# V of the first 256 tokens in float32 from unnormalised tokens, and dt beside V in one product

## The chip, the cores and the metric

The kernel runs on one core of a Trainium2 chip. The metric is the device time of one execution in microseconds: before the change 1092.85 us, the median of three runs (1092.71 to 1092.87).

## What is computed

The reference is one layer of an encoder trunk with 512 tokens of width 1024, in float32: a mixing sub-layer and an MLP, each between RMSNorms. The change touches only the beginning of the first sub-layer:

```python
h = rmsnorm(x, pre_mix_norm[l])          # x * rsqrt(mean(x*x) + EPS) * gain, per token
proj = h @ w_in[l]                       # 1024 x 9792
z, xbc, dt_raw, q, k, v, gates = split_cols(proj, IN_SPLITS)
...
dt = jax.nn.softplus(dt_raw.astype(jnp.float32).reshape(Bsz, S, 2, G, R)
                     + dt_bias.astype(jnp.float32).reshape(2, G, R))
...
out = jnp.einsum('bngrqk,bnkgd->bnqgrd', p.astype(v.dtype), vb)
```

v has 256 columns, dt 64 (32 heads in each of two directions). A token's norm is one number per token, and the gain one per input channel.

## The kernel before, in words

**Splitting.** Most products run on TensorE in float32r, a faster form with fewer bits. To keep float32's accuracy each operand is split into a high part (a cast, ACT, L495) and a low part (the rest, POOL or DVE, L499), and `mm3` (L426) adds three products: high with high, high with low, low with high. A plain float32 product (`mm` with float32 operands) is recorded as two weight loads and two MATMUL records. h, the normalised tokens transposed to channels x tokens, is kept split, as eight pairs of tiles of 128 channels x 512 tokens.

**Quanta.** `build` (L1596) lists the work of TensorE as quanta, each with its chunks of weights. `prefetch` (L503) issues a chunk's load from SP (L475) and its split (L495, L499) some chunks ahead: raw weights (`wr`) have 3 buffers, split ones (`wh`, `wl`) have 3. Functions set at a quantum's index (`at`, `later`) are emitted between quanta. At the end `chain` (L519) hands all instructions to a planner, which goes through them with estimated costs and due times and fixes the order on each engine; within an engine, the order of the built program is kept by the hardware. Loads issued from SP go through eight completion semaphores (shared with ACT's two at the start), so the ninth waits until the first has landed.

**The start** (`start`, L591). ACT issues the loads of the identity (`ident`) and the gain (`g`). TensorE does 18 products of a zero tile (`WARM`) that nothing reads, then turns the gain into a column `gT`. `start_tokens` (L620) loads a group of tokens, sums their squares (ACT L635 and DVE L636, half each), takes the inverse root on POOL (L638, L639), scales them (ACT L640, DVE L641), transposes them on TensorE (L424 through `tr`), and splits them with the gain into h (ACT L445, DVE L446). It is called for token group 0 (a group is 128 tokens) at once, with six more unread products (`DUMMY`, x with itself), for group 1 and for groups 2 and 3 together a little later. Loads on SP stand in this order: group 0, the two chunks of V's weights (512 KB each), groups 1, 2 and 3, dt's weights, `vec`, `hot`, K's first weights, the constants `cst`, and so on.

**V, dt, K.** `tm` (L567) makes four quanta for V, one per token group, each 24 split products 256 wide, with tokens as the output's rows; `v_done` copies two groups at once into V. Then `dt_quantum` (L722): dt's 64 columns, high and low part side by side as 128 columns, times both parts of h (16 products 512 wide), gives dt as columns x tokens; a quantum later four float32 products with a folding matrix (`cst,dtr`) turn it back and add the parts; `dt_math` (L746) adds the bias and goes on. Then two quanta for K (24 split products 512 wide each, `cm` L548), and Q. `vectors` (L685) and `bias_rows` (L704) put two transposes and one float32 product (`ps<-hot,vec`) between.

Of the kernel before, what the change touches and what calls it, by code (L numbers as in the profile page):

```python
# [10 lines left out]
F32 = mybir.dt.float32  # L11
# [20 lines left out]
FAR, AHEAD = (2,3,5,6,8,9,11,12,), 5  # L32

BACK = 3
WARM = 18
DUMMY = 6
COLD = 7000.0
RATE, LAND = 260, 2500

# [39 lines left out]
class Slots:  # L79
# [13 lines left out]
    def put(self, *tiles):  # L93
        for t in tiles:
            self.free.append(self.slot.pop(id(t))[0])
# [266 lines left out]
class Trunk:  # L362
# [169 lines left out]
    def run_quanta(self):  # L532
        c = released = 0
        for self.now, q in enumerate(self.quanta):
            n = len(q.chunks)
            self.prefetch(released + SPL + RAW - 2, SPL, released)
            self.emit(self.now)
            q.run([self.parts.pop(c + i) for i in range(n)])
            self.emit(self.now + 0.5)
            c += n  # L540
            released += q.release
        self.now += 1
        while self.acts:
            self.now = min(self.acts)
            self.emit(self.now)
        self.chain()
# [17 lines left out]

        return Quantum(chunks, run)

    def tm(self, c, done):  # L567

        src = lambda k0: self.d_w_in[k0 * 128:(k0 + 4) * 128, c:c + 256].rearrange("(k p) n -> p k n", p=128)
        chunks = [(src(k0), 4, 256, "vpvp") for k0 in (0, 4)]  # L570
        held, ps = [], []

        def step(t):
            def run(parts):
                held.extend(parts)
                if t % 2 == 0:
                    ps.append(self.bank("ps"))
                tok = slice(t * 128, (t + 1) * 128)
                for k in range(8):
                    wh, wl = held[k // 4]  # L580
                    h = self.h[k]
                    self.mm3(ps[-1][:, t % 2 * 256:t % 2 * 256 + 256], (h[0][:, tok], h[1][:, tok]),
                             (wh[:, k % 4], wl[:, k % 4]), k == 0, k == 7)
                if t % 2:
                    done(t // 2, ps[-1])
            return run

        return [Quantum([] if t else chunks, step(t), 2 if t == 3 else 0) for t in range(NT)]


    def start(self):  # L591
        nc = self.nc
        get, put = self.slots.get, self.slots.put
        self.ident = self.const("ident", [128, 128])
        nc.scalar.dma_start(self.ident, self.d_cst[:, :128])
        g = get("g", (128, 128))
        nc.scalar.dma_start(g[:8], self.d_pre_mix_norm[0].rearrange("(k p) -> k p", p=128))
        self.mhalf = self.const("mhalf", [128, 1])
        nc.vector.memset(self.mhalf, -0.5)
# [3 lines left out]
        zero = get("zero", (128, 128))  # L603
        nc.vector.memset(zero, 0.0)
        pg = self.bank("ps")
        for _ in range(WARM):
            self.mm(pg[:, 128:256], zero, zero, True, True)
        put(zero)
        self.tr(pg[:, :8], g[:8, :])
        nc.vector.tensor_copy(self.gT, pg[:, :8])  # L610
        put(g)
        self.dummy = self.bank("ps")
        self.h = [(get("h", dtype=F32R), get("h", dtype=F32R)) for _ in range(8)]
        self.start_tokens([0])
        self.prefetch(2, 1)
        self.at(1, lambda: self.start_tokens([1]))
        self.at(2, lambda: self.start_tokens([2, 3]))
        self.at(1, self.later_constants)

    def start_tokens(self, ts):  # L620

        nc = self.nc
        get, put = self.slots.get, self.slots.put
        n = len(ts)
        ps = [self.bank("pp" if 0 in ts else "ps") for _ in range(2 * n)]
        at = lambda k, i=0, j=n: ps[k % (2 * n)][:, (k // (2 * n) * n + i) * 128:(k // (2 * n) * n + j) * 128]
        xs = {t: [get("x") for _ in range(2)] for t in ts}
        for t in ts:
            for j, x in enumerate(xs[t]):
                nc.sync.dma_start(x, self.d_x[0, t * 128:(t + 1) * 128, j * 512:(j + 1) * 512])  # L630
        for i, t in enumerate(ts):
            xt = xs[t]
            junk = [get("junk") for _ in range(2)]
            ssq, r = self.ssq0[:, 2 * t:2 * t + 2], self.rst0[:, t:t + 1]
            nc.scalar.activation(junk[0], xt[0], AF.Square, scale=D ** -0.5, accum_out=ssq[:, 0:1])  # L635
            nc.vector.tensor_tensor_reduce(junk[1], xt[1], xt[1], 1.0 / D, EPS, ALU.mult, ALU.add, ssq[:, 1:2])  # L636
            put(*junk)
            nc.gpsimd.tensor_tensor(r, ssq[:, 0:1], ssq[:, 1:2], op=ALU.add)  # L638
            nc.gpsimd.tensor_tensor(r, r, self.mhalf, op=ALU.pow)  # L639
            nc.scalar.activation(xt[0], xt[0], AF.Copy, scale=r)  # L640
# [3 lines left out]
            if t == 0:  # L644
                for _ in range(DUMMY):
                    self.mm(self.dummy[:, :128], xt[1][:, :128], xt[1][:, :128], True, True)
# [57 lines left out]
    def bias_rows(self):  # L704

        nc = self.nc
        get, put = self.slots.get, self.slots.put
        hot = get("hot")
        nc.sync.dma_start(hot[:33], self.d_hot)
        ps = self.bank("ps")  # L710
        self.mm(ps[:16, :], self.vec[:33, 256:], hot[:33], True, True)
        rows = get("rows")
        nc.vector.tensor_copy(rows[:16], ps[:16, :])
        self.brow = self.dp.tile([16, 512], F32, name="brow")
        nc.sync.dma_start(self.brow, rows[:16])
        put(hot, rows, self.vec)
        self.row = self.const("row", [128, 176])
        self.bcast_row(self.row, self.d_row, 176)
        self.sink = self.row[:, 128:144]


    def dt_quantum(self):  # L722


        w = self.d_w_in

        def run(parts):
            ps = self.bank("pp")
            for k in range(8):
                for i, h in enumerate(self.h[k]):  # L730
                    self.mm(ps, parts[0][:, k], h, k + i == 0, k + i == 8)
            raw = self.slots.get("dtr")
            self.nc.scalar.copy(raw, ps)

            def flip():
                pt = self.bank("ps")
                for t in range(NT):
                    self.mm(pt[:, t * 64:(t + 1) * 64], raw[:, t * 128:(t + 1) * 128], self.fold, True, True)
                self.slots.put(raw)
                self.dt_math(pt)  # L740

            self.later(1, flip)

        return Quantum([(w[:, C_DT:C_DT + 64].rearrange("(k p) n -> p k n", p=128), 8, 64, "both")], run)

    def dt_math(self, ps):  # L746
# [6 lines left out]
        w = [get("dtw", (128, 4, 64)) for _ in range(6)]  # L753
        v, e, r, s2, p, al = w
        nc.vector.tensor_tensor(v, ps[:, :256].rearrange("p (c h) -> p c h", c=4),
                                bias[:, 0].unsqueeze(1).to_broadcast([128, 4, 64]), op=ALU.add)

        nc.scalar.activation(e, v, AF.Abs)
        nc.scalar.activation(e, e, AF.Exp, scale=-1.0)
# [49 lines left out]
    def kv_quanta(self):  # L809
        nc = self.nc  # L810
        get = self.slots.get
        self.KH, self.KL, self.V = [], [], []

        def k_done(ps):
            for j in range(2):
# [7 lines left out]
                self.KH.append(KH)  # L823
                self.KL.append(KL)

        def v_done(t2, ps):
            V = get("V", (128, 2, 256))
            nc.scalar.copy(V, ps.rearrange("p (t c) -> p t c", t=2))
            self.V.append(V)

        hh = lambda: self.h
        return self.tm(C_V, v_done) + [self.cm(self.d_w_in, C_K + 128 * i, hh, k_done) for i in range(2)]

    def backward(self, ap):

# [760 lines left out]
    def build(self):  # L1596
# [5 lines left out]
        self.at(4, self.vectors)  # L1602
        self.at(4, self.bias_rows)
        self.at(8, self.scan_constants)
# [73 lines left out]
```

## Time and profile before

| | |
|---|---|
| median of three runs | 1092.85 us (1092.71 to 1092.87) |
| profiled execution, first to last instruction (span) | 1090.1 us |
| TensorE busy (PE) | 1080.1 us, 99% |
| VectorE, ScalarE, GpSimd busy | 740.1, 642.9, 794.5 us |
| moved by DMA | 132.31 MB, 121 GB/s in the mean |

The profile gives no time of its own for the profiled execution beyond the span; the difference of 2.75 us between span and median lies before the first and after the last instruction. PE is TensorE's products, PEld its weight loads, DVE VectorE, ACT ScalarE, POOL GpSimd, SP the queue that issues nearly all loads. In a timeline row stand start, length, engine, line, operation, output<-inputs, form and count, and in brackets the idle time of the engine before it and what ended it. The length of a matmul record runs from its start to its modelled end, so back-to-back records overlap; the step between starts is what one costs. Tile names carry no buffer numbers: `h<-pp,gT` is the split of h, `wr` raw weights, `wh` and `wl` their parts.

### The profile page before, as it was taken

How to read it: one execution, taken by the hardware profiler on the slowest of the kernel's cores; microseconds unless marked ns; L12 is line 12 of the kernel's file. 1: busy time of each engine (PE TensorE's matmuls, PEld its weight loads, DVE VectorE, ACT ScalarE, POOL GpSimd, SP SyncE). 2: the span in 40 equal slices, each digit the busy share in tenths (PEclk: the TensorE clock that was granted, in tenths of full speed). 3: DMA queues.
4: the chain of work that ended last, by engine and by line, in shares of the span. 5: the costliest groups of instructions: out<-in, count | busy, mean ns of one | idle time of the engine just before them, and what ended most of it. 6: DMA issues, size and time to landing. Idle time of an engine off the chain costs nothing.

```text
span 1090.1 us, 16770 instructions
## 1 busy us (share of the span) xinstructions
PE 1080.1 (99%) x5631; PEld 906.1 (83%) x5631; DVE 740.1 (68%) x1288; ACT 642.9 (59%) x1379; POOL 794.5 (73%) x977
## 2 busy tenths in 40 slices
PE   9999999999999999999999999999999999999997
PEld 8888888888888888888888888889888888888885
DVE  5567788687788687778788753334672583583698
ACT  6566777686776777676769633323554544544552
POOL 3546657557668888988999876521588898898994
PEclk9999999999999999999999999999999999999998
DMA  7434433634354536354655554534322422424222
GB/s 205 127 95 129 117 94 95 157 90 118 100 123 127 145 101 174 97 141 134 162 138 140 145 173 121 165 103 155 92 70 71 153 74 83 154 74 147 90 97 77
DMA packets 209209, 132.31 MB, mean 121 GB/s; under 512 B 10538, under 2 KB 192042, under 8 KB 209123
## 3 DMA queue, kind: packets, MB, share of 16 engines
q1 hardware_dynamic: 208963, 131.18, 42.6%
q8 instruction: 44, 0.72, 0.3%
q14 instruction: 42, 0.34, 0.1%
q10 hardware_dynamic: 160, 0.07, 0.0%
HBM read 126.69 MB, written 4.52 MB: 120 GB/s over the span
## 4 chain that ended last, share of the span: by engine, by line
PE 98%; DVE 0%; DMA 0%; ACT 0%; issue 0%; POOL 0%; DVEq 0%; POOLq 0%; SPq 0%
PE pp L420 69%; PE ps L420 25%; PE ps L424 3%; DMA rb<-csT 0%; DVEq L1674 0%; DVE ag L1586 0%; DVE h L446 0%; POOLq L1674 0%; ACT h L445 0%; ACT wh L495 0%; SPq L1101 0%; PE pp L424 0%; POOL ssq L1164 0%; ACT x L640 0%; DVE acc L1564 0%
## 5 line engine op out<-in xcount | busy, mean ns | idle before, releaser
L499 POOL TENSOR_TENSOR wl<-wr,wh 128x256 fp32r<-128x256 f32 (+1 forms) x504 | 426.0, 873 | 153.5 <-ACT wh L495 141.7
L420 PE MATMUL pp<-h,wh 128*128 128x512 f32 (+1 forms) x1728 | 527.9, 388 | 0.0
L420 PEld LDWEIGHTS pp<-h,wh 128*128 128x128 f32 x1728 | 318.9, 188 | 64.1 <-issue 1.9
L420 PE MATMUL pp<-h,wl 128*128 128x512 f32 (+1 forms) x856 | 332.3, 388 | 0.0
L495 ACT CAST wh<-wr 128x1024 fp32r<-128x1024 f32 (+1 forms) x133 | 138.9, 1044 | 144.6 <-PE pp L420 125.2
L420 PEld LDWEIGHTS pp<-h,wl 128*128 128x128 f32 x856 | 160.9, 188 | 32.5 <-issue 0.5
L1512 POOL TENSOR_TENSOR wl<-wd,wh 128x256 fp32r<-128x256 f32 x158 | 131.1, 865 | 11.7 <-ACT wh L1509 11.6
L1509 ACT CAST wh<-wd 128x512 fp32r<-128x512 f32 x82 | 47.5, 621 | 32.8 <-PE ps L420 15.5
L420 PE MATMUL ps<-wl,fh 128*128 128x512 f32 x164 | 63.9, 390 | 0.0
L420 PE MATMUL ps<-wh,fl 128*128 128x512 f32 x164 | 63.8, 389 | 0.0
L420 PE MATMUL ps<-wh,fh 128*128 128x512 f32 x164 | 63.8, 389 | 0.0
L1379 DVE SCALAR_TENSOR_TENSOR pp<-pp,r 128x512 f32<-128x512 f32 (+1 forms) x31 | 17.6, 567 | 66.3 <-ACT r L1376 66.3
L1120 ACT ACTIVATE n<-cb,tables 128x128 f32<-128x128 f32 x128 | 49.5, 394 | 17.1 <-DVE cb L1111 16.6
L952 DVE SCALAR_TENSOR_TENSOR u<-pp,cv,u 128x510 f32<-128x510 f32 (+1 forms) x64 | 47.7, 745 | 4.5 <-ACT u L948 3.4
L420 PE MATMUL pp<-yh,wl 128*128 128x512 f32 x128 | 49.8, 390 | 0.0
L420 PE MATMUL pp<-yh,wh 128*128 128x512 f32 x128 | 49.7, 389 | 0.0
L420 PE MATMUL pp<-yl,wh 128*128 128x512 f32 x128 | 49.6, 389 | 0.0
L1121 ACT ACTIVATE m<-cb,tables 128x128 f32<-128x128 f32 x128 | 49.3, 393 | 0.3 <-DVE cb L1111 0.2
L1116 ACT ACTIVATE rf<-rf,tables 128x128 f32<-128x128 f32 x128 | 42.7, 396 | 11.2 <-DMA rf<-csT 11.1
L1156 POOL TENSOR_TENSOR w<-w,E 128x256 f32<-128x256 f32 x48 | 37.9, 803 | 13.1 <-DVE w L1152 11.8
L1050 POOL TENSOR_TENSOR xd<-x,tables 128x256 f32<-128x256 f32 x48 | 33.0, 705 | 17.8 <-ACT x L975 12.8
L884 ACT ACTIVATE P<-P,mx 128x384 f32<-128x384 f32 (+1 forms) x64 | 35.3, 554 | 15.6 <-DVE mx L881 15.3
(271 smaller groups left out, 2163.1 us busy)
## 6 DMA issues: line engine op xcount, KB each, us to landing
wr<-in_w_in SPq DMA_DIRECT2D x76, 512.0 KB, 4.0
wr<-in_w_mlp_in SPq DMA_DIRECT2D x32, 512.0 KB, 4.2
wd<-in_w_mlp_out SPq DMA_DIRECT2D x64, 256.0 KB, 6.3
rf<-csT SPq DMA_DIRECT2D x32, 256.0 KB, 4.8
rb<-csT SPq DMA_DIRECT2D x32, 256.0 KB, 3.7
wr<-in_w_ssd_out SPq DMA_DIRECT2D x14, 512.0 KB, 3.9
E<-csE SPq DMA_DIRECT2D x96, 64.0 KB, 4.2
x<-in_x SPq DMA_DIRECT2D x16, 256.0 KB, 4.2
```

The costliest lines, as they stand in the source:

```text
L420: self.nc.tensor.matmul(out, lhsT, rhs, start=start, stop=stop, skip_group_check=more)
L495: self.nc.scalar.copy(hi[:, :m], raw)
L499: engines[e].tensor_tensor(lo[:, c], raw[:, c], hi[:, c].bitcast(F32), op=ALU.subtract)
L884: nc.scalar.activation(p[:, :w], p[:, :w], AF.Exp, bias=mx[:, n:n + 1], accum_out=sm[:, n:n + 1])
L952: nc.vector.scalar_tensor_tensor(u[:, a:e], ps[:, a + d:e + d], self.wtap(t, b), u[:, a:e], op0=ALU.mult, op1=ALU.add)
L1050: nc.gpsimd.tensor_tensor(v4(xd[:, d * 256:(d + 1) * 256]), v4(xs(c)), by_dir(self.coef, c)[:, d].unsqueeze(2).to_broadcast([128, 4, 64]), ...
L1116: nc.scalar.activation(v4(rf)[:, h], v4(rf)[:, h], AF.Identity, bias=ncs[:, 0, h:h + 1])
L1120: nc.scalar.activation(v4(n)[:, h], cb[:, 0], AF.Copy, scale=dt[:, 0, h:h + 1])
L1121: nc.scalar.activation(v4(m)[:, h], cb[:, 1], AF.Copy, scale=dt[:, 1, h:h + 1])
L1156: nc.gpsimd.tensor_tensor(wc, wc, E[:, d], op=ALU.add)
L1509: nc.scalar.copy(hi, src)
L1512: (nc.vector if q == 512 else nc.gpsimd).tensor_tensor(lo[:, c], src[:, c], hi[:, c].bitcast(F32), op=ALU.subtract)
```

## The change

V and dt now share one set of weights: three chunks of 2, 3 and 3 blocks of 128 channels, each with V's 256 and dt's 64 columns side by side (320 wide), loaded by two DMAs.

Token groups 0 and 1 are transposed raw (`raw_tokens`), and their eviction from PSUM multiplies only by the gain, into `xg`. Their V and dt are plain float32 products, `xg` with the unsplit weights, 16 in all, 320 wide; the token's inverse norm is applied when V and dt are evicted (`done`: ACT for V, DVE for dt, with the bias). Group 1's transposes are issued between the first chunk's products for group 0 and those for group 1. The weights are split as well (ACT the high part, DVE and POOL the low part in turns), for groups 2 and 3.

h of groups 0 and 1, which K, Q and all others need, is made later by `scale_tokens`: two products of a matrix of ones with a diagonal of the inverse norms give a tile with the norms along the row; DVE multiplies `xg` by it (eight times, 256 wide), ACT casts the high part, POOL subtracts the low part.

Groups 2 and 3 go through `start_tokens` as before, and their V and dt are 48 split products 320 wide. dt comes out with tokens as rows, so that `dt_quantum`, its flip and its 64 columns times 512 tokens are gone. `WARM` goes from 18 to 6, on a tile of ones, and `DUMMY` away. The load of `row` (dt's bias among others) moves ahead of `vec` and `hot`; the loads of group 1 move ahead of the second and third chunk of weights. The first call of `prefetch` takes one raw chunk fewer.

In the changed program's order on ACT, group 1's V eviction stands ahead of the scaling of group 3, and the eight splits of groups 2 and 3 ahead of the cast of K's first weights; on POOL the eight low parts of groups 0 and 1 stand between the four subtractions of K's first weights.

```diff
-WARM = 18
-DUMMY = 6
+WARM = 6
+V_CHUNKS = ((0, 2), (2, 5), (5, 8))
...
-            self.prefetch(released + SPL + RAW - 2, SPL, released)
+            self.prefetch(released + SPL + RAW - 2 - (self.now == 0), SPL, released)
...
+    def v_quanta(self):
...
+            def loads():
+                r = self.wp.tile([128, 1024], F32, tag="wr", name=self.name("wr"), bufs=RAW)
...
+                for c, n, at in ((C_V, 256, 0), (C_DT, 64, 256)):
+                    nc.sync.dma_start(raw[0][:, :, at:at + n],
+                                      w[k0 * 128:k1 * 128, c:c + n].rearrange("(k p) n -> p k n", p=128))
+
+            def make():
+                hi, lo = (t[:, :kk * 320].rearrange("p (k n) -> p k n", k=kk) for t in self.weight_parts())
+                nc.scalar.copy(hi, raw[0])
+                for k in range(kk):
+                    e = nc.vector if k % 2 == 0 else nc.gpsimd
+                    e.tensor_tensor(lo[:, k], raw[0][:, k], hi[:, k].bitcast(F32), op=ALU.subtract)
+                return raw[0], hi, lo
...
+        def done(t, ps):
+            bias = self.row[:, :64]
+            if t < 2:
+                r = self.rst0[:, t:t + 1]
+                nc.scalar.activation(self.V[0][:, t], ps[:, :256], AF.Copy, scale=r)
+                nc.vector.scalar_tensor_tensor(self.dtv[:, t], ps[:, 256:320], r, bias, op0=ALU.mult, op1=ALU.add)
+            else:
+                nc.scalar.copy(self.V[1][:, t - 2], ps[:, :256])
+                nc.vector.tensor_tensor(self.dtv[:, t], ps[:, 256:320], bias, op=ALU.add)
...
+        def plain(parts):
...
+            for (k0, k1), (raw, _, _) in zip(V_CHUNKS, parts):
+                for t in range(2):
+                    if (k0, t) == (0, 1):
+                        self.raw_tokens(1)
+                    for k in range(k0, k1):
+                        self.mm(ps[t][:, :320], self.xg[k][:, tok(t)], raw[:, k - k0], k == 0, k == 7)
...
+        def rest(c):
+            def run(_):
...
+                for t in (2, 3):
+                    for k in range(k0, k1):
+                        hi, lo = self.h[k]
+                        self.mm3(late[t - 2][:, :320], (hi[:, tok(t)], lo[:, tok(t)]), (wh[:, k - k0], wl[:, k - k0]),
+                                 k == 0, k == 7)
...
+    def raw_tokens(self, t):
...
+        for k in range(8):
+            self.tr(ps[k // 4][:, k % 4 * 128:(k % 4 + 1) * 128], xt[k // 4][:, k % 4 * 128:(k % 4 + 1) * 128])
+        for k in range(8):
+            dst, src = self.xg[k][:, t * 128:(t + 1) * 128], ps[k // 4][:, k % 4 * 128:(k % 4 + 1) * 128]
+            if k < 4:
+                nc.scalar.activation(dst, src, AF.Copy, scale=self.gT[:, k:k + 1])
+            else:
+                nc.vector.tensor_scalar(dst, src, self.gT[:, k:k + 1], None, op0=ALU.mult)
+        self.token_scale(t, xt)
...
+    def scale_tokens(self, ones, xg):
...
+        for t in range(2):
+            dg = get("dg", (128, 128))
+            nc.gpsimd.tensor_scalar(dg, self.ident, self.rst0[:, t:t + 1], None, op0=ALU.mult)
+            self.mm(rb[:, t * 128:(t + 1) * 128], ones, dg, True, True)
...
+        for k in range(8):
+            x = hf[k // 2][:, k % 2 * 256:(k % 2 + 1) * 256]
+            nc.vector.tensor_tensor(x, rb[:, :256], self.xg[k], op=ALU.mult)
+            hi, lo = (a[:, :256] for a in self.h[k])
+            nc.scalar.copy(hi, x)
+            nc.gpsimd.tensor_tensor(lo, x, hi.bitcast(F32), op=ALU.subtract)
...
-        kv = self.kv_quanta()
-        self.add(*kv[:4], self.dt_quantum(), *kv[4:])
+        self.add(*self.v_quanta(), *self.kv_quanta())
```

More of the change, by code (lines that the diff above doesn't have):

```diff
@@ L586, in step @@
             return run
-        return [Quantum([] if t else chunks, step(t), 2 if t == 3 else 0) for t in range(NT)]
+        return [Quantum([chunk(*c) for c in V_CHUNKS], plain, 0)] + [Quantum([], rest(c), 1) for c in range(3)]
     def start(self):
@@ new lines, in token_scale @@
+    def token_scale(self, t, xt):
+        nc = self.nc
+        get, put = self.slots.get, self.slots.put
+        junk = [get("junk") for _ in range(2)]
+        ssq, r = self.ssq0[:, 2 * t:2 * t + 2], self.rst0[:, t:t + 1]
+        nc.scalar.activation(junk[0], xt[0], AF.Square, scale=D ** -0.5, accum_out=ssq[:, 0:1])
+        nc.vector.tensor_tensor_reduce(junk[1], xt[1], xt[1], 1.0 / D, EPS, ALU.mult, ALU.add, ssq[:, 1:2])
+        put(*junk)
+        nc.gpsimd.tensor_tensor(r, ssq[:, 0:1], ssq[:, 1:2], op=ALU.add)
+        nc.gpsimd.tensor_tensor(r, r, self.mhalf, op=ALU.pow)
+        return r
@@ L624, in start_tokens @@
         n = len(ts)
-        ps = [self.bank("pp" if 0 in ts else "ps") for _ in range(2 * n)]
+        ps = [self.bank(tag) for tag in ("pp", "pp", "ps", "ps")]
         at = lambda k, i=0, j=n: ps[k % (2 * n)][:, (k // (2 * n) * n + i) * 128:(k // (2 * n) * n + j) * 128]
[L627 to L630, printed above, removed]
+        xs = [self.load_tokens(t) for t in ts]
         for i, t in enumerate(ts):
[L632 to L639, printed above, removed]
+            xt = xs[i]
+            r = self.token_scale(t, xt)
             nc.scalar.activation(xt[0], xt[0], AF.Copy, scale=r)
@@ L716, in bias_rows, with dt_math @@
         put(hot, rows, self.vec)
[L717 to L746, printed above, removed]
+    def dt_math(self):
         nc = self.nc
@@ L824, in k_done @@
                 self.KL.append(KL)
[L826 to L829, printed above, removed]
         hh = lambda: self.h
[L832 removed]
+        return [self.cm(self.d_w_in, C_K + 128 * i, hh, k_done) for i in range(2)]
     def backward(self, ap):
```

90 lines of the change are left out of this document (54 added, 36 removed).

## The prediction

> **What bounds the kernel now.** I read the page first, then the busy time by stretches, the waits of PE, and the timeline of the first 60 us. From the page: busy time, the clock row, and the chain that ended last.
>
> ```profile
> PE 1080.1 (99%) x5631; PEld 906.1 (83%) x5631; DVE 740.1 (68%) x1288; ACT 642.9 (59%) x1379; POOL 794.5 (73%) x977
> ...
> PEclk9999999999999999999999999999999999999998
> ...
> PE 98%; DVE 0%; DMA 0%; ACT 0%; issue 0%; POOL 0%; DVEq 0%; POOLq 0%; SPq 0%
> ```
>
> TensorE is 99% of the span and 98% of the chain. The stretches show where the last per cent lies (columns: length, then busy time and instructions of PE, PEld, DVE, ACT, POOL; clock; DMA):
>
> ```profile
> 0.00:21.00 21.00, 19.18 (x122) 17.09 (x122) 12.03 (x36) 14.36 (x35) 8.60 (x17) 1.00 0.84 244
> 21.00:70.00 49.00, 49.00 (x256) 41.18 (x256) 29.53 (x63) 28.91 (x56) 23.19 (x32) 1.00 0.39 108
> 70.00:200.00 130.00, 130.00 (x775) 110.82 (x774) 98.97 (x224) 92.30 (x222) 78.89 (x102) 1.00 0.41 111
> 400.00:800.00 400.00, 399.64 (x2024) 334.71 (x2023) 261.44 (x375) 227.40 (x478) 290.49 (x346) 1.00 0.48 135
> ```
>
> From 21 us on PE does not rest. So any PE work taken out, or any earlier start of the useful products, moves the end by as much. Before 21 us much of "busy" is filler:
>
> ```profile
> 1.03 6.64 PE L420 MATMUL ps<-zero 128*128 128x128 f32 x36 [1.03 <-DVE mhalf L599]
> ...
> 8.08 1.04 PE L424 MATMUL pp<-ident,x 128*128 128x128 f32 x8
> 8.95 1.28 PE L420 MATMUL ps<-x 128*128 128x128 f32 x10
> 9.99 0.36 PE L420 MATMUL ps<-wh,h 128*128 128x256 f32 x1
> ```
>
> The first product whose result is used starts at 9.99 us. The start is the whole matter: I compare the time at which the first product of K begins, since nothing but PE work follows it and the two programs have the same products from there.
>
> **That mark in the kernel before.**
>
> ```profile
> 20.75 1.40 PE L420 MATMUL pp<-h,wh 128*128 128x512 f32 x4
> ...
> 23.82 0.40 PE L420 MATMUL pp<-h,wh 128*128 128x512 f32 x1
> ...
> 25.92 0.40 PE L420 MATMUL ps<-wh,h 128*128 128x256 f32 x2
> 26.16 0.28 PE L420 MATMUL ps<-wl,h 128*128 128x256 f32 x1
> 26.28 0.40 PE L420 MATMUL ps<-wh,h 128*128 128x256 f32 x2
> ...
> 29.21 1.03 PE L420 MATMUL ps<-hot,vec 33*16 33x512 f32 x2
> 30.17 3.26 PE L420 MATMUL pp<-h,wh 128*128 128x512 f32 x13
> 33.27 0.39 PE L420 MATMUL pp<-h,wl 128*128 128x512 f32 x1
> ...
> 34.18 0.62 PE L420 MATMUL pp<-h,wh 128*128 128x512 f32 x2
> ...
> 34.86 0.62 PE L420 MATMUL pp<-h,wh 128*128 128x512 f32 x2
> ...
> 38.26 1.00 PE L420 MATMUL ps<-cst,dtr 128*128 128x64 f32 x8
> 39.07 0.71 PE L420 MATMUL pp<-h,wh 128*128 128x512 f32 x2
> ...
> 55.75 0.34 PE L420 MATMUL ps<-KH,Q 128*128 128x384 f32 x1
> 55.93 0.34 PE L420 MATMUL ps<-KL,Q 128*128 128x384 f32 x1
> ```
>
> dt's product has 16 matmuls: 4, 1, and 11 of the 13 at 30.17; the other two are K's. Three 512-wide products take 34.86 - 34.18 = 0.68 us, 0.227 each, so K begins at 33.27 - 0.45 = 32.8. dt's flip, which the change drops, sits later, 39.07 - 38.26 = 0.8. Mark before: 32.8 + 0.8 = **33.6 us**.
>
> **What is removed and added on PE, in full-clock time.** Removed: 96 V products of (26.28 - 25.92) / 3 = 0.12, 11.5 us; dt's 16 of 0.227, 3.6; the flip, 0.8. Together 15.9. The 18 warming products and the 6 behind the first transposes are filler.
>
> Added: 16 float32 products 320 wide, which no row shows. The 10 records at 8.95 are five 128-wide float32 products at (9.99 - 8.95) / 5 = 0.21 us; the 512-wide one at 29.21 took at most 0.96 with its change of type. Per column that is 1.63 to 1.88 ns, so 0.52 to 0.60 for 320; I take 0.54, nearer the back-to-back row: 8.6 us (8.3 to 9.6). Then 48 split products 320 wide, between 0.12 (256) and 0.18 (384, the step 55.75 to 55.93): 0.149, 7.2 us. Two 128-wide ones for the scale rows, 0.4. Together 16.2. The arithmetic on PE is thus a draw (+0.3). A gain can only come from starting earlier and waiting less: the old stretch from 9.99 to 33.6 holds 23.6 us for 15.9 + 24 transposes (2.6) + vec and hot (1.3) = 19.8 us of work.
>
> **When the new products can start.** What lands when (engine rows that a load ended, then the DMA rows):
>
> ```profile
> 3.72 0.63 ACT L635 ACTIVATE junk<-x 128x512 f32<-128x512 f32 x1 [0.66 <-DMA x<-in_x]
> 4.48 0.69 DVE L636 CUSTOM_DVE_ANT_0 junk<-x 128x512 f32<-128x512 f32 x1 [3.49 <-DMA x<-in_x]
> 7.10 1.05 ACT L495 CAST wh<-wr 128x1024 fp32r<-128x1024 f32 x1 [0.20 <-DMA wr<-in_w_in]
> ```
>
> ```profile
> 3.90 0.99 SPq L630 DMA_DIRECT2D x<-in_x  x2
> ```
>
> ```profile
> 1.03:7.60 6.57, 6.57 (x36) 6.45 (x36) 1.19 (x3) 3.23 (x5) 0.74 (x2) 1.00 0.85 263
> 7.60:10.00 2.40, 2.40 (x23) 2.38 (x22) 1.99 (x5) 1.50 (x4) 1.77 (x2) 1.00 1.02 377
> ```
>
> Token 0's halves land at 3.72 and 4.48 and stay first on SP's queue. The third x load waited for ident, so ident lands by 3.90. Before, 512 KB of weights stood behind them and landed at 7.10; now the first chunk is 320 KB, so I put it near 5.6 (7.10 at worst). The second chunk ends after 1.94 MB (constants 68 KB, tokens 1 MB, weights 800 KB): 263 GB/s x 6.57 us = 1.73 MB are through by 7.6, the rest at 377 GB/s by 8.2, and with some 0.4 to land 8.6. The third, 480 KB more, by about 10.3 with its 256-byte rows. Tokens 2 and 3 follow at 11 to 13, where they used to come before.
>
> The raw tokens need no norm chain now (sums, POOL's power, scaling: 4.48 to 6.9), only the gain column. But the clock matters:
>
> ```profile
> 1.62 1.27 PE L420 MATMUL ps<-zero 128*128 128x128 f32 x5
> ...
> 6.73 0.94 PE L420 MATMUL ps<-zero 128*128 128x128 f32 x7
> ```
>
> Five records step by (1.27 - 0.42) / 4 = 0.21 us early, seven by (0.94 - 0.28) / 6 = 0.11 later: PE begins at half speed, though the granted clock reads 1.00. 36 records in 6.57 us put the change near 5.9 us, 4.8 us after the first product. The new program issues 6 warming products (1.03 to 3.6 at 0.43 each), waits for ident, and does 8 transposes (0.11 each at full speed, the 8 at 8.08; 0.22 at half) with the gain's: 3.95 to about 6.0. The first two float32 products run from 6.0.
>
> I let the pause at 3.6 start the count of 4.8 us anew and the transposes count, so that full speed comes at 3.95 + 4.8 = 8.8 us. The walk: two products at 1.07 to 8.1; token 1's transposes to 9.3; its evictions on ACT (0.3 each) pace the next two to 10.5; then 12 at 0.54, all weights landed, to **17.0**.
>
> **From there to K.** ACT, DVE and POOL durations (timeline, then groups by shape):
>
> ```profile
> 6.18 0.72 ACT L640 ACTIVATE x<-x,rst 128x512 f32<-128x512 f32 x1 [1.74 <-POOL rst L639]
> ...
> 21.33 0.86 ACT L445 ACTIVATE h<-ps,gT 128x256 fp32r<-128x256 f32 x2
> ...
> 10.69 2.11 POOL L499 TENSOR_TENSOR wl<-wr,wh 128x256 fp32r<-128x256 f32 x2 [0.62 <-ACT wh L495]
> ...
> 28.80 5.60 POOL L499 TENSOR_TENSOR wl<-wr,wh 128x256 fp32r<-128x256 f32 x8 [9.38 <-ACT wh L495]
> ```
>
> ```profile
> L495 ACT CAST wh<-wr 128x1024 fp32r<-128x1024 f32 x4 | 4.2, 1047 | 3.4 <-PE ps L420 3.2 <-DMA wr<-in_w_in 0.2
> ```
>
> ACT's order is the new wait: V of token 1 (after the last float32 product) stands ahead of token 3's scaling, so the scaling ends at 17.0 + 0.2 + 0.4 + 0.7 = 18.3. Token 2's transposes and the scale rows fill PE until then; token 3's follow, and the first split of h (0.43) frees PE at 19.2. Then 7.2 + 1.3 + 0.3 for changes of type: K begins at **28.0**. The splits (8 x 0.43) outrun PE, which uses 0.9 us per k. The weight casts and the row load hide beside the float32 products.
>
> POOL is late next. Its queue holds token 0 and 1's low parts interleaved with K's: 11 subtractions behind K's cast, which ends 8 x 0.43 + 1.05 after 18.8, at 23.3. At 0.70 (28.80) they end at 31.0; K needs the last at 28.0 + 7 x 0.68 = 32.8. Hidden with 1.8 us to spare.
>
> Sum: 33.6 - 28.0 = 5.6 us. The profiled span is 1090.1, the median of the runs 1092.85, 2.75 above it; what lies around the span is the same in both, so the time is 1092.85 - 5.6 = **1087.2 us** (span 1084.5).
>
> **The rivals.**
>
> Early clock: the warming products and transposes count together and full speed comes at 5.9 as before. Then two products end at 7.1, token 1's evictions on ACT decide (8.05, after a cast and a square), float32 ends at 15.95, K at 26.9: 1086.2. For it: PE is nearly as busy as before. Against: a gap at 3.6 and transposes instead of products.
>
> Late clock: transposes do not count, and token 1's break the products. They stay at half speed to 9.9, and the 4.8 us run from there to 14.7: 4.5 products at 1.07, 9.5 at 0.54, float32 ends at 19.8, K begins at 30.8: 1090.0. For it: the trace had 4.8 us of unbroken products before the change of speed, and the new program breaks them twice. Against: no row shows a transpose that delays it. [...]
>
> POOL: with DVE active beside it a subtraction took 2.11 / 2 = 1.05 us (10.69). Then 11 end at 34.9, 2.1 after K's need: 1089.3. For it: DVE works on the same tiles. Against: its operands there are mostly in PSUM, and the row at 28.80 has eight at 0.70.
>
> Slower: float32 products at half speed throughout. 14 at 1.07 from 9.9 end at 24.9, K at 35.9, 2.3 past the old mark: 1095.2. It decides if full speed comes after about 20 us (5.6 us lost at half a microsecond for each makes 11 us beyond 8.8). For it: fewer warming products and pauses for loads. Against: a dozen products in a row from 10.5 are as dense as what raised the clock before.
>
> **How the numbers follow.** Forecast 0.40 (1086.7 to 1088.2), early clock 0.27, late clock 0.14, POOL 0.08, half speed throughout 0.06, and 0.05 for several small delays that leave 1091 to 1094. About 0.2%, 2.2 us, is what a measurement can tell from no change: faster 0.89, same 0.05, slower 0.06. Weights landing at 7.1 instead of 5.6 cost up to 1 us, float32 products at 0.60 another 0.9; with the clock cases the range is 1085.3 to 1090.2.
>
> **What would show it.** The first float32 product near 6 us, the step of its records 0.54 (half speed) turning to 0.27 by 9 to 11; the last before 18; the first 320-wide split product near 19; K's first product near 28, and PE without a rest from there. Wrong if PE waits for POOL in K, if the second weight chunk lands after 10, or if the step stays at 0.54.

## The result and the profile after

Over 20 runs of each kernel the changed one takes 1091.01 us (1089.11 to 1092.70), the one before 1092.59 us (1090.82 to 1093.25): the ratio is 0.9985, with a 95% interval of 0.9979 to 0.9992. The gain is 1.6 us where 5.6 were forecast, and the time lies outside the range. The profiled execution's span is even a little longer than before, 1090.8 against 1090.1 us. But it is the execution of 1092.70 us, the longest of the 20. The profiled executions whose own time is on record take 1.8 to 2.2 us more than their spans. So the execution profiled before took about 1092 us, and some 0.6 to 0.9 of the 2.75 us between its span and the median are no time outside the instructions: that execution was shorter than the median. Single executions of the changed kernel lie up to 3.6 us apart, so one profile shows where time goes, and the runs show how much.

From the page of the changed kernel, TensorE's share and the chain that ended last:

```profile
PE 1076.4 (99%) x5559; PEld 899.5 (82%) x5559; DVE 748.1 (69%) x1290; ACT 640.3 (59%) x1378; POOL 799.2 (73%) x985
...
PE 63%; DVE 1%; DMA 0%; issue 0%; DVEq 0%; POOL 0%; POOLq 0%; SPq 0%; ACT 0%
```

PE is busy 3.7 us less than before, with 72 instructions fewer, and yet nothing of it shows in the span. The chain adds up to 64% only: followed back from the end, it leaves TensorE near 390 us, at a wait that the profile of before doesn't have. The table of PE's waits names it (total, times, longest):

```profile
PE ps L424 <- DVE tables L844: 1.8, 1, 1.8
PE ps L420 <- DMA wr<-in_w_in: 1.4, 1, 1.4
PE ps L420 <- DVE m L1181: 1.2, 1, 1.2
...
PE ps L420 <- DVE pT L959: 0.3, 1, 0.3
```

The second belongs to the start, which the forecast walked through. The others lie behind it: `tables` (L844) is the copy of dt's running sums out of PSUM, `m` and `pT` are tiles of the mixing. First the start, in the timeline of PE:

```profile
4.59 0.99 PE L424 MATMUL pp<-ident,x 128*128 128x128 f32 x7
6.93 1.31 PE L420 MATMUL ps<-wr,xg 128*128 128x320 f32 x4 [1.36 <-DMA wr<-in_w_in]
...
9.14 7.80 PE L420 MATMUL ps<-wr,xg 128*128 128x320 f32 x28
...
19.98 0.42 PE L420 MATMUL ps<-wh,h 128*128 128x320 f32 x1 [0.45 <-ACT h L445]
...
28.55 0.63 PE L420 MATMUL pp<-h,wh 128*128 128x512 f32 x2
```

K begins at 28.55 us. Against the old mark of 33.6 that is a gain of 5.05 us, nearly the 5.6 of the forecast. So the start did what it should, and the gain is lost later. Where, the timeline of PE 17 us further on shows:

```profile
45.01 1.12 PE L420 MATMUL ps<-dtw,cst 128*128 128x128 f32 x6
47.95 0.63 PE L424 MATMUL ps<-ident,tables 128*64 128x128 f32 x4 [1.82 <-DVE tables L844]
48.59 0.90 PE L420 MATMUL pp<-h,wh 128*128 128x512 f32 x2
...
52.27 0.70 PE L420 MATMUL pp<-h,wh 128*128 128x512 f32 x2
```

After dt's sums (`ps<-dtw,cst`) PE stands still for 1.82 us. Behind the pause nine products of Q (three times two with `wh` and one with `wl`; the rows between are left out) take 52.27 - 48.59 = 3.68 us, 0.41 each instead of 0.227: 1.64 us lost. The stretches say why (length; busy time of PE, PEld, DVE, ACT, POOL; granted clock; DMA):

```profile
46.00:48.00 2.00, 0.18 (x2) 0.05 (x2) 1.26 (x4) 1.92 (x5) 0.00 (x0) 1.00 0.86 253
...
49.00:52.41 3.41, 3.41 (x10) 2.67 (x9) 1.84 (x4) 3.31 (x7) 0.71 (x2) 0.50 0.04 10
```

The granted clock falls to 0.50 behind the pause. A tile that both programs use later, `m`, carries the count on. Its products start at these first and last times, before and after:

```profile
L420 PE MATMUL ps<-m,x x128: 272/273/323, 146.8 to 388.6; 128*64 128x128 f32 x128
```

```profile
L420 PE MATMUL ps<-m,x x128: 272/273/324, 145.5 to 389.7; 128*64 128x128 f32 x128
```

Of the 5.05 us, 146.8 - 145.5 = 1.3 are left at the first of them: 3.75 are gone, of which pause and half clock make 3.46. By the last one another 2.4 are gone; the waits for m and pT in the table above are 1.5 of these, and the other 0.9 have no row that I can name. Part of them is spread: from the first to the last of these products the first profile of before takes 241.8 us, and the two later ones, taken further below, 242.2.

**Why PE stands still at 46 us.** The timelines of VectorE, GpSimd and ScalarE, one after the other:

```profile
30.42 0.92 DVE L831 TENSOR_SCALAR dtw<-dtw 128x256 f32<-128x256 f32 x1 [1.04 <-ACT dtw L821]
...
36.02 6.25 DVE L829 SCALAR_TENSOR_TENSOR dtw<-dtw,dtw 128x256 f32<-128x256 f32 x7
...
44.07 0.84 DVE L834 SCALAR_TENSOR_TENSOR dtw<-tables,row 128x256 f32<-128x256 f32 x1
44.84 1.27 DVE L883 TENSOR_TENSOR KL<-pp,KH 64x512 fp32r<-64x512 f32 x2
46.75 0.69 DVE L883 TENSOR_TENSOR KL<-pp,KH 64x512 fp32r<-64x512 f32 x1 [0.64 <-ACT KH L882]
47.47 0.42 DVE L844 COPY tables<-ps 128x256 f32<-128x256 f32 x1
```

```profile
31.16 9.81 POOL L499 TENSOR_TENSOR wl<-wr,wh 128x256 fp32r<-128x256 f32 x12
41.27 3.37 POOL L499 TENSOR_TENSOR wl<-wr,wh 128x256 fp32r<-128x256 f32 x4 [0.30 <-ACT wh L495]
```

```profile
34.22 0.58 ACT L882 CAST KH<-pp 64x512 fp32r<-64x512 f32 x1 [3.38 <-PE pp L420]
...
45.54 0.58 ACT L884 CAST KH<-pp 64x512 fp32r<-64x512 f32 x1 [4.35 <-DVE KL L883]
```

VectorE works through dt's whole softplus chain, L831 to L834, from 30.42 to 44.9 without a break. K's first product is done at 34.2 (ScalarE casts its high part then), but its low part, `KL` on VectorE, stands behind the chain and starts at 44.84; ScalarE waits 4.35 us for it. The sums' copy L844 stands behind three such KL and starts at 47.47, 1.3 us after the sums' end on PE (45.01 + 1.12). In the kernel before, VectorE's order was another one, and dt's chain began 11 us later (L768 there is L831 here), since it followed a quantum of its own and not V:

```profile
39.30 0.42 DVE L755 TENSOR_TENSOR dtw<-ps,row 128x256 f32<-128x256 f32 x1 [8.34 <-PE ps L420]
39.64 0.67 DVE L820 TENSOR_TENSOR KL<-pp,KH 64x512 fp32r<-64x512 f32 x1
41.39 0.29 DVE L768 TENSOR_SCALAR dtw<-dtw 128x256 f32<-128x256 f32 x1 [1.08 <-ACT dtw L758]
42.00 0.69 DVE L820 TENSOR_TENSOR KL<-pp,KH 64x512 fp32r<-64x512 f32 x1 [0.32 <-ACT KH L819]
...
46.20 4.03 DVE L766 SCALAR_TENSOR_TENSOR dtw<-dtw,dtw 128x256 f32<-128x256 f32 x5
```

There K's low parts stood between the steps of the chain.

### The profile page after: what moved, and what is told of

It reads as the page before. It is cut to its first block, busy times and chain, and to the rows that moved or that the text cites. A ratio compares the mean times of both kernels' runs of the same rounds, so it can differ in the third digit from the quotient of the medians.

```text
span 1090.8 us, 16649 instructions
## 1 busy us (share of the span) xinstructions
PE 1076.4 (99%) x5559; PEld 899.5 (82%) x5559; DVE 748.1 (69%) x1290; ACT 640.3 (59%) x1378; POOL 799.2 (73%) x985
## 4 chain that ended last, share of the span: by engine, by line
PE 63%; DVE 1%; DMA 0%; issue 0%; DVEq 0%; POOL 0%; POOLq 0%; SPq 0%; ACT 0%
PE pp L420 45%; PE ps L420 17%; PE ps L424 1%; DMA rb<-csT 0%; DVE m L1180 0%; DVE m L1181 0%; DVEq L1731 0%; DVE ag L1644 0%; POOLq L1731 0%; DVE rf L1175 0%; SPq L1159 0%; POOL ssq L1222 0%; DVE acc L1622 0%; ACT sh L437 0%; POOL frs L1647 0%
## 5 line engine op out<-in xcount | busy, mean ns | idle before, releaser
L495 ACT CAST wh<-wr 128x1024 fp32r<-128x1024 f32 x131 | 136.5, 1042 | 141.7 <-PE pp L420 117.8
L1178 ACT ACTIVATE n<-cb,tables 128x128 f32<-128x128 f32 x128 | 49.0, 390 | 16.3 <-DVE cb L1169 16.0
```

What stands on the lines that cost most here:

```text
L495: self.nc.scalar.copy(hi[:, :m], raw)
L1178: nc.scalar.activation(v4(n)[:, h], cb[:, 0], AF.Copy, scale=dt[:, 0, h:h + 1])
```

## The experiments

The theories at first: **A**, the rows of the sums (four transposes of `tables`) are placed too close behind the sums; **B**, K's evictions are late, and a shift of the rows only moves the pause. All edits are to the changed kernel unless said otherwise.

### The rows one place later

```diff
-        self.later(3, rows)
+        self.later(4, rows)
```

> The changed kernel with one number changed: the transposes of dt's running sums (L424, ps<-ident,tables) are emitted one quantum later, so that 24 products of Q and eight of the scores stand between them and the sums (ps<-dtw,cst). Theory A: TensorE's pause of 1.82 us at 46 us (it waits for the copy L844 on DVE) and the half speed from 48.6 to 52.3 us (9 products in 3.68 us instead of 2.04, 1.6 us) come from that place in the order, and are what took back most of the 5 us won at the first K product. Then the pause and the half speed are both gone, K still begins at 28.5, and the time is 1.8 to 3.4 us below the changed kernel, about 1088. Rival B: the loss lies elsewhere (DMA or DVE work pushed back as a whole), and the pause only moves: another wait of about the same length turns up within the next 20 us and the time stays within 0.7 us of the changed kernel's 1091.

1090.25 us (1088.66 to 1092.39); the ratio to before on the same chip is 0.9987 (0.9978 to 0.9996), as for the changed kernel. PE and ScalarE in its timeline:

```profile
44.56 1.12 PE L420 MATMUL ps<-dtw,cst 128*128 128x128 f32 x6
48.13 0.73 PE L420 MATMUL pp<-h,wh 128*128 128x512 f32 x2 [2.46 <-ACT KH L884]
```

```profile
45.09 0.58 ACT L884 CAST KH<-pp 64x512 fp32r<-64x512 f32 x1 [4.37 <-DVE KL L883]
```

With the rows out of the way PE stands still all the same, 2.46 us now, since Q's second product needs the PSUM buffer that K's first one still holds (`pp` has three). A fell as to the place; the pause belongs to K's evictions.

### The pause filled

```diff
+            pf = self.bank("ps")
+            for _ in range(8):
+                self.mm(pf[:, :128], al[:, 0:2], self.ones, True, True)
```

> The changed kernel with eight unread float32 products, 128 wide (0.21 us each, 1.7 us), put right behind dt's running sums, where TensorE pauses for 1.82 us. They compute nothing that is used. Theory A: the pause itself sets off the half speed, so the wait stays (K at 28.5, the transposes at about 48) but the products behind it run at 0.23 us each; the time is up to 1.6 us below the changed kernel, and the spread of its runs (1089.1 to 1092.7) shrinks to the lower half. Rival C: the half speed has another cause (a limit reached by the products themselves): it stays at 48.6, and the time is that of the changed kernel or a little above it.

Eight float32 products behind the sums, which nothing reads, keep PE busy. 1089.74 us (1088.14 to 1091.51), ratio 0.9981 (0.9973 to 0.9990). Stretches:

```profile
46.00:48.00 2.00, 1.95 (x17) 1.49 (x15) 1.80 (x3) 1.90 (x5) 0.00 (x0) 1.00 0.58 175
48.00:50.00 2.00, 2.00 (x9) 1.63 (x10) 1.53 (x5) 1.95 (x5) 0.00 (x0) 1.00 0.03 8
```

The clock stays at 1.00, though the useful work waits as long as before. The ratio is 0.0006 lower than that of the run above, 0.65 us, which the intervals don't tell apart; they allow anything from no gain to about 2 us. What half clock costs in the mean of the runs is not settled by this. It is not the whole loss: without it the ratio is still 0.9981, where the forecast would be 0.995. That the spread would shrink did not come true.

### No warming at the start

```diff
-WARM = 6
+WARM = 0
```

> The changed kernel without its six warming products (WARM 0). In the changed kernel the seven transposes at 4.59 already step by 0.12 us, full speed. If the six products bring that about, then without them the transposes and the first float32 products run at half speed: the two or four products in front of token 1's take 0.54 us more each, the first K product moves from 28.5 to 29 or 30, and the time rises by 0.5 to 1.5 us. If the speed at the start does not matter, because the first product waits for its weights until 6.93 us anyway, K stays at 28.5 and the time stays within 0.5 us.

1091.57 us (1090.87 to 1092.99), ratio 0.9998 (0.9989 to 1.0007). K begins at 27.94 in its profile, no later than with warming, and the pause at `tables` is there with 1.8 us, with the half clock behind it. Neither case of the expectation came: K is no later, and yet the ratio is 0.0013 (1.4 us) above the changed kernel's, with intervals that just overlap. Which part of it the missing products cost, this one profile doesn't show.

### A shorter chain

```diff
-        for n in (15, 13, 11, 9, 7, 5, 3):
+        for n in (5, 3):
```

> The changed kernel with five of the seven polynomial terms of dt's softplus left out (L829, five DVE instructions of 0.89 us beside POOL, 4.5 us; dt is less exact). The planner then puts the running sums 9 products earlier and 20 products between them and the transposes. Theory A with its second half (what made dt late is the length of its DVE chain, whose instructions take 0.84 to 0.92 us beside POOL's subtractions instead of 0.43 alone): no pause at 46, no half speed, the time 1.8 to 3.4 us below the changed kernel, like the kernel whose transposes come a quantum later. Rival B: the time stays within 0.7 us of the changed kernel.

Softplus has five polynomial terms fewer, VectorE five instructions. 1086.26 us (1086.04 to 1087.12), ratio 0.9951 (0.9938 to 0.9963): 5.4 us below before, the size of the forecast. VectorE:

```profile
35.37 1.73 DVE L829 SCALAR_TENSOR_TENSOR dtw<-dtw,dtw 128x256 f32<-128x256 f32 x2
...
39.65 0.67 DVE L883 TENSOR_TENSOR KL<-pp,KH 64x512 fp32r<-64x512 f32 x1
```

K's low part starts 5.2 us earlier, and no pause is left. But that leaves two theories: **D**, K's evictions only stand in the wrong place, behind the chain; or the chain is too long wherever it stands.

### The same work in another order

dt's sums and their rows set one, two and three places later in the list of quanta, with nothing else changed (the diff shows the first; 4 and 5 follow, then 5 and 6); beside them the changed kernel once more.

```diff
-        self.later(2, sums)
-        self.later(3, rows)
+        self.later(3, sums)
+        self.later(4, rows)
```

> The changed kernel once more, unaltered, to stand beside the three other runs on the same chip. Both theories expect the ratio of the first measurement, 0.998 to 0.999 (some 1.6 us below before), TensorE's pause of about 1.8 us near 46 us for the sums' copy on VectorE, and about 3.5 us of half clock behind it. If the pause is absent in this profile, it is no fixed part of the program.

> dt's sums one place later in the program and the rows of the sums one place later too; nothing else changes. VectorE's order thereby gets K's low parts between the polynomial's terms and not behind dt's whole chain. Theory D (K's evictions stand behind dt's uninterrupted chain on VectorE, so that neither a PSUM buffer nor the sums' copy is ready at 46 us): no pause over 0.5 us between 44 and 56 us, clock 1.00 there, 1086 to 1088 us, some 3 to 5 us below the changed kernel. The rival (the chain is simply too long: whoever needs its end waits wherever it stands, and only its shortening helped): the pause returns some 4 to 10 us later, half clock behind it, 1090 to 1091 us.

> dt's sums and their rows two places later; nothing else changes. The first of K's low parts now stand ahead of the polynomial on VectorE, and the sums behind the first products of the mixing. Theory D: no pause between 44 and 60 us, 1086 to 1087.5 us, as in the run with the shortened chain (1086.26). The rival of a chain too long: a pause where the rows are first needed, near 50 to 60 us, 1089 to 1091 us. If the time stays at 1090 without any pause before 60 us, the loss lies elsewhere, in the wait near 389 us or behind it.

> dt's sums and their rows three places later; K's low parts stand on VectorE as in the run before this one. Theory D: the same time as two places later, within 1 us, since the order of K's evictions is the same. If it is over 1 us slower, something behind the sums (the scan's tables) is the next to be late, and the wait shows between 55 and 80 us.

On one chip, with the kernel before at 1091.82 us there:

| | median (lowest to highest) | ratio to before |
|---|---|---|
| changed kernel again | 1090.60 (1088.19 to 1093.32) | 0.9988 (0.9979 to 0.9997) |
| one place later | 1088.24 (1087.39 to 1088.83) | 0.9963 (0.9950 to 0.9975) |
| two places | 1088.01 (1087.65 to 1088.31) | 0.9961 (0.9948 to 0.9973) |
| three places | 1087.61 (1087.13 to 1088.75) | 0.9960 (0.9948 to 0.9973) |

VectorE and one of the stretches, three places later:

```profile
36.42 0.68 DVE L883 TENSOR_TENSOR KL<-pp,KH 64x512 fp32r<-64x512 f32 x1
37.02 1.29 DVE L829 SCALAR_TENSOR_TENSOR dtw<-dtw,dtw 128x256 f32<-128x256 f32 x2
38.34 0.69 DVE L883 TENSOR_TENSOR KL<-pp,KH 64x512 fp32r<-64x512 f32 x1
...
45.44 0.82 DVE L834 SCALAR_TENSOR_TENSOR dtw<-tables,row 128x256 f32<-128x256 f32 x1
```

```profile
46.00:48.00 2.00, 2.00 (x11) 1.65 (x10) 0.94 (x2) 1.94 (x4) 0.85 (x1) 1.00 0.46 125
```

The chain is no shorter and ends at 46.3, later than in the changed kernel. But `KL` starts at 36.42 instead of 44.84, PE does not pause and the clock holds. D holds, and the rival of a chain too long falls: its end is not needed that early, only VectorE is. The edit moves two things, the sums on PE and, through the planner, K's evictions on VectorE; no run moves one without the other. That the evictions matter by themselves the run with only the rows moved shows: there PE waited 2.46 us for the buffer that they free, not for the sums. The order is worth 1090.60 - 1087.61 = 3.0 us here, with no work taken away. In the changed kernel's own second profile the pause is there with 1.8 us, and no half clock behind it.

### Further profiles, and the wait for m

The kernel before two times more, the changed one a third time, and three places later on another chip:

> The kernel before once more, unaltered, for a second profile. Asked: does TensorE's wait for m near 385 to 390 us (0 in the first profile of before, 0.2 to 1.7 us in the profiles of the variants) belong to the change? If it does, it is absent here again; if it is the varying length of the transfer behind it, 0 to 1.7 us can show here too. And when does the clock rise: at 5.9 us again, or anywhere between 4 and 10 us?

> A third profile of the kernel before, with the same two questions: the wait for m (0, or 0 to 1.7 us), and the time of the clock's rise (5.9, or varying).

> A third profile of the changed kernel. The pause of 1.8 us for the sums' copy near 46 us is expected again. Behind it the first profile showed 3.7 us of half clock and the second none: either can come. The clock's rise at the start came at 4.6 us in one and at 9 us in the other profile.

> dt's sums and rows three places later, as in the run of that name, a second time on a chip of its own. Theory D: no pause between 44 and 60 us again, 4.0 to 5.4 us below before: the more, the earlier the clock rises at the start (rise at 9 us: about 4.2; at 5 to 7 us: about 5.2). The rival (chain too long) would bring a pause back; 1090 us or more.

Single runs: before 1091.03 and 1092.11, the changed kernel 1089.05. Three places later: 1087.09 us (1086.36 to 1088.89), ratio 0.9958 (0.9945 to 0.9972), with no pause from 44 to 60 us, and 4.7 us below before (1091.82 on this chip as well). This order beats both kernels, and nothing of the computation is left out in it.

The wait for m is absent in all three profiles of before and present in all those of the changed program, with 0.2 to 1.5 us as the longest, whatever the order. It stands behind a row norm whose numbers go through HBM, and that takes longer. Counted from the norm's first copy (L1178, in the changed program L1236), SP issues the last load after 16.6 to 16.9 us in the three profiles of before and after 16.7 to 17.9 in those of the changed program; it lands 6.0 to 6.3 us after its issue before, and 6.1 to 7.1 after the change. VectorE, on which m comes later, waits for it 3.2 to 3.3 us before, and 3.3 to 5.3 us after. SP in a profile of before (the second), then of three places later (the second):

```profile
364.00 1.87 SPq L1101 DMA_DIRECT2D E<-csE  x3
365.98 0.54 SPq L1185 DMA_DIRECT2D rrow<-rcol  x1
```

```profile
359.73 2.99 SPq L1159 DMA_DIRECT2D E<-csE  x3
362.81 0.54 SPq L1243 DMA_DIRECT2D rrow<-rcol  x1
```

Three loads of E ahead of it on SP's queue take 1.87 us in all three profiles of before, and 1.87 to 3.00 in those of the changed program. The changed program has issued three loads more up to there, and loads take turns at eight completion semaphores (in the first profile of each kernel all issues, 475 before and 478 after, go to the same eight, in turn but for two at the start). Theory **E**: the turn decides. Two runs, five loads of one number each in the order three places later (three and five make a full turn), and three in the kernel before:

```diff
         self.nc.sync.dma_start(cst, self.d_cst[:, 128:])
+        ph = self.const("ph", [1, 8])
+        for i in range(5):
+            self.nc.sync.dma_start(ph[:, i:i + 1], self.d_cst[:1, 128 + i:129 + i])
```

> The run with dt's sums three places later, and five loads of one number each that nothing reads, behind the constants: the changed program issues three loads more than before up to here, and with five more every later load meets the same of the eight completion semaphores as before. Theory E: the wait for m near 389 us hangs on that turn of the loads. Then the three E loads ahead of rstd's take 1.9 us on SP as in all three profiles of before (2.4 to 3.0 in the two of this variant), the wait for m is gone, and the time is 0.5 to 1.5 us less than without them, some 1086 us. The rival: the turn does not matter, the wait stays between 0.2 and 1.7 us, and the time stays at 1087 to 1088 us.

> The reverse: the kernel before with three loads of one number each that nothing reads, so that its later loads meet the semaphores of the changed kernel. Theory E: E's three loads take up to 3.0 us instead of 1.9, a wait for m of up to 1.7 us appears near 389 us, and the time rises by 0.5 to 1.5 us. The rival: neither, and the time stays within 0.5 us of before.

With five loads: 1089.40 us (1087.67 to 1090.74), ratio 0.9968 (0.9959 to 0.9977); the three E loads take 2.95 us and the wait for m is 1.5. Before with three: 1092.62 (1091.72 to 1094.19), ratio 1.0004 (0.9995 to 1.0012); E takes 1.87 and no wait for m appears. E fell in both directions. Why the loads are issued later there, and land later, stays open; so does what the five loads cost in the first run (0.9968 against 0.9958 and 0.9960, intervals overlapping).

## Why the prediction was wrong

**The step that failed** is the premise that the mark at K settles the time, "since nothing but PE work follows it and the two programs have the same products from there". The products are the same; the work of VectorE beside them is not in the same order. dt's chain begins at 30.42 instead of 41.39, and the program set all of it ahead of K's evictions. "PE without a rest from there" was named as what would show the forecast right, and it is what did not come. Of the rivals, none held this: POOL in K was the only wait behind the mark that I priced, and POOL was in time. The chance of 0.05 for several small delays covers the measured time (1091 to 1094), but names no mechanism. The diff says that dt_quantum goes and dt comes beside V; I followed that on PE, ACT and POOL up to K, but did not ask what VectorE does with dt once it is there.

**The start, term by term.**

- The sum on PE: the float32 products 320 wide were taken at 0.54 us; 14 of them, 28 records, fill the 7.80 us from 9.14 on, and their starts step by 0.54 each. The split ones were taken at 0.149: 0.147 by their steps in the timeline (three in 0.44). Both right.
- The first weights were put at 5.6 us, 7.1 at worst. They landed at 6.93 in the first profile, and at 5.73 to 6.53 in others where PE waited for them.
- The clock: forecast at 8.8, rival at 5.9. In the first profile the seven transposes at 4.59 step by (0.99 - 0.27) / 6 = 0.12. The trace also keeps records of the granted clock, each with its start and length; the first one, at full speed, begins at 4.62, in the early rival's way and earlier still. In three other profiles of the changed program it begins at 4.4 to 5.1, in three at 7.1 to 7.2 (one of them without warming), and in the four of the table above and the one with five loads at 9.2 to 10.2. So early and late both happen, with the same program, and 8.8 never. Where full speed came by 7.2, K began at 27.8 to 28.1 (28.55 where the weights were late); where it came at 9.2 or later, at 29.1 to 29.4.
- That the forecast of 28.0 lies among the first of these is partly luck. For an early clock it had 26.9. Where full speed came by 5.1, the float32 products ended 0.4 to 0.5 us later than that sum had it (1.0 in the first profile), with waits for weights in each, and K came 11.3 to 11.65 us behind them, not 11.0. The late rival's premise that transposes do not count is shown by no run. Without warming, the transposes at 4.03 are PE's first work, only 1.0 us of products follows them, and full speed still came at 7.21.
- POOL was to be 1.8 us ahead of K's need. PE shows no wait for `wl` in K: right.

**What is left of the 5.6 us.** With K's evictions in place the runs give 4.2 and 4.7 us. The profile of the first of them has K at 29.07, 4.5 us before the mark, and a wait for m of 0.3; its span is 1090.1 - 1085.7 = 4.4 us shorter. So the working of the start carries through to the end once nothing behind it stalls.

**How the loss is made up.** Shown: the pause goes with the order, and some 2.4 to 3.0 us of time with it; in the one profile with PE kept busy the granted clock stays at 1.00. The half clock comes in some executions only: in the first profile and in two variants with the pause, not in the second and third of the changed kernel.

When it comes, the five profiles with a rest of 1.8 us or more show. Their records of the clock run in steps of 3.413 us: in the first profile full speed lasts from 4.62 to 49.00, 13 steps, with the rows one place later from 4.39 to 48.76, 13 steps, and without warming from 7.21 to 48.17, 12 steps; each time half clock follows for one step, 3.41 us. Counted on from the rise, the rest lies inside one step in these three (46.13 to 47.95 in the step from 45.58 to 49.00, for one), and PE is busy for 0.95 to 1.59 us of it. In the two profiles without half clock a step ends within the rest (at 47.45 in the rest from 46.94 to 48.76, and at 46.04 in that from 45.37 to 47.19), and PE is busy for 2.10 us or more of each step. In the filled variant the wait (45.49 to 47.31) lies inside one step, 44.67 to 48.08, and with PE busy throughout no half clock follows. The first profile, then the second of the changed kernel:

```profile
45.58:49.00 3.42, 1.59 (x10) 0.88 (x9) 2.62 (x5) 3.31 (x6) 0.00 (x0) 1.00 0.59 156
```

```profile
47.45:50.86 3.41, 2.10 (x10) 1.60 (x11) 2.79 (x5) 3.29 (x7) 0.00 (x0) 1.00 0.42 124
```

So in these profiles the same pause costs half a step more (1.64 us in the first) or nothing more, by the time at which the clock happened to rise.

The times of single executions agree with this. One step at half clock is 0.5 x 3.41 / 1090 = 0.0016 of the mean granted clock. Of the changed kernel's first 20 executions, six have a mean clock of 0.997 and take 1091.8 us in the mean, and 14 have 0.998 and take 1090.3; with the rows one place later, five at 0.996 or 0.997 take 1091.4 and six at 0.998 or 0.999 take 1089.6. Without the pause it isn't so: of 27 executions of the kernel before on the same chip, seven at 0.997 take 1091.5 and the other 20 take 1091.9, and the one execution of the filled variant at 0.997 is its shortest. That half clock makes these differences is argued from this and not tested one by one. It is not the whole spread: the filled variant has no pause, and its 11 runs still lie 3.4 us apart.

## What to carry to other kernels

When a change lets a result come earlier, look at what its consumers do to the queue of the engine they run on: here an early dt put 14 us of softplus ahead of the evictions that free PSUM. An engine at 69% can still stop the one at 99% if its order is wrong, and the cure was the order, with no work taken away. A mark in the timeline settles the time only if every engine's order behind it is the same in both programs; compare the orders behind the mark before trusting it.

## What the hardware showed beside this

**VectorE beside GpSimd.** Most of the chain's steps with two operands in SBUF take twice as long while POOL subtracts, 0.84 to 0.89 us in the first profile instead of 0.42 to 0.43 without it. With sums and rows one place later, VectorE and then POOL:

```profile
36.77 4.37 DVE L829 SCALAR_TENSOR_TENSOR dtw<-dtw,dtw 128x256 f32<-128x256 f32 x5
41.07 0.67 DVE L883 TENSOR_TENSOR KL<-pp,KH 64x512 fp32r<-64x512 f32 x1
41.67 0.86 DVE L829 SCALAR_TENSOR_TENSOR dtw<-dtw,dtw 128x256 f32<-128x256 f32 x2
42.57 0.43 DVE L830 SCALAR_TENSOR_TENSOR dtw<-dtw,dtw 128x256 f32<-128x256 f32 x1
```

```profile
31.92 9.83 POOL L499 TENSOR_TENSOR wl<-wr,wh 128x256 fp32r<-128x256 f32 x12
45.35 2.13 POOL L499 TENSOR_TENSOR wl<-wr,wh 128x256 fp32r<-128x256 f32 x3 [3.61 <-ACT wh L495]
```

Until POOL ends at 41.75, a polynomial term takes 4.37 / 5 = 0.87 us, afterwards 0.43; `KL`, with one operand in PSUM, keeps to 0.67 to 0.69 throughout. One step (L825, 0.45 in the first profile) kept its speed beside POOL. A step with a single operand slowed down as well: L827 takes 0.72 in the first profile, its counterpart in the kernel before (L764), with POOL at rest, 0.29. Which steps escape, and why, stays open. In the changed kernel POOL is busy for nearly all of the chain (31.16 to 44.64, but for 0.30 us), and a polynomial term takes 6.25 / 7 = 0.89 us there. That this made the chain longer is argued from the 0.43 above; no run tried the chain without POOL.
